# The pool mixer's bias by one matmul per bank, and GpSimd's tensor operations moved to VectorE

## The chip, the cores and the metric

The kernel runs on one core of one Trainium2 chip. The metric is device time in microseconds (us): the time of an execution of the whole program. The profile shows one execution by the hardware profiler; its span reaches from the first to the last instruction. The engines are PE (TensorE, matmuls), with its weight loads as PEld; DVE (VectorE); ACT (ScalarE); POOL (GpSimd); SP (SyncE), which issues the DMAs.

## The reference

One layer of a decoder trunk over x of 1024 tokens by 1024 columns, float32:

```python
h = rms_norm(x, norm_mix_g)                  # per token
for gi, w_len in enumerate((2, 4, 8, 16)):   # 4 groups of 256 columns
    d[gi] = mean of h over the last w_len tokens - h     # fewer at the start
y = scale * (einsum('bsgc,gcd->bsgd', d, pool_w) + pool_b)
x = x + y
f = (silu(gate) * val) @ ffn_w_out           # val, gate: halves of
                                             # causal_conv3(rms_norm(x, norm_ffn_g) @ ffn_w_in) + conv_b
out = x + f                                  # hidden width 2816 (twice)
```

The change concerns the term `scale * pool_b` in y, and sums on the way to the first feed-forward product.

## The kernel before, in words

The tokens go in eight tiles of 128. A loop of twelve passes (j = 0 to 11) is a software pipeline over them. In pass j it writes:

- mixer_norm(j): the window matrices, scaled by the tile's 1/rms (DVE, L148).
- mixer_window(j - 1): 8 matmuls of 128x128 (L152, each shown as two) give the windowed differences in PSUM (psd). A correction of the first 16 tokens (L187, L189), then a split into a rounded part dh (ACT, L190) and a rest dl (DVE, L191). Between them stands L181: GpSimd adds the scaled bias to the tile xs[j] itself, in place, once the window matmuls have read it.
- in pass 1 also mixer_edges (the 16 tokens ahead of each tile) and mixer_weights: pool weights times gain and scale (DVE, L168, 8 pieces), split into wph (ACT, L173) and wpl (DVE, L174).
- mixer_out(j - 2): 24 matmuls of 128x256 (L206) into psy, two banks: per group of 256 columns six matmuls, dh by wph, dh by wpl, dl by wph, for two halves of the contraction. Then L209 (DVE) adds psy and xs[j]; the sum x1 is stored to DRAM (L210), its statistics are taken (L131 to L138, ACT and DVE), and a diagonal matrix of 1/rms is built (L213).
- ffn_operand(j - 4): 8 matmuls of x1 by that diagonal (L229, each shown as two) transpose and scale the tile; seven of eight column blocks are brought out by ACT (L234), one by DVE (L236), into n2f. The first feed-forward product is a Strassen-Winograd scheme, so it needs sums of quarters of n2f. Tiles 0 to 3 are only split (L251 on ACT, L252 on DVE). For tiles 4 to 7 the difference b11 = b12 - b11 is formed (DVE, L263) and split as operand T1, and two more differences, b12 = b22 - b12 (L246) and b21 = b21 - b22 (L247), are formed by GpSimd.

The statistics of the coming tiles, preparation steps for the first product's left operands (prep_event, with splits by L69 and L70 and sums by L263 and L266) and its first three products (event) are written into the same loop. load_in(0) and load_in(1), which bring w_in, stand in passes 4 and 6. After the loop come the operands B22, T2, T3 and T4; for T4, GpSimd adds t1 to t4 in two halves (L432). Then all 22 blocks of the first product run, seven products of 12 matmuls of 128x512 each (L295), and then the second product (L567), 924 matmuls of 128x512.

GpSimd's other work is at the start: memsets and masks of the window matrices (L88 to L103), and L121, which multiplies the bias rows, brought to all partitions by a DMA (L117), by the scale rows (L112).

The order on each engine is not that of the text alone. The framework plans it when the kernel is built, from the order of writing, its own costs and the buffers that are free; the waits are put in by it. Each engine then runs its queue in that order. `issue_after(marks[...])` keeps some preparation steps behind L209 of a given tile. float32 is multiplied as two or three products of parts rounded to fp32r, which is why tensors are split into a rounded part and a rest.

Of the kernel before, what the change touches and what calls it, by code (L numbers as in the profile page):

```python
# [7 lines left out]
F32 = mybir.dt.float32  # L8
F32R = mybir.dt.float32r
BF16 = mybir.dt.bfloat16  # L10
AF = mybir.ActivationFunctionType
ALU = mybir.AluOpType
PSUM = bass.MemoryType.PSUM

P = 128
# [8 lines left out]
WINDOWS = (2, 4, 8, 16)  # L24
HALO = 16
EPS = 1e-6
# Columns of the packed per-partition parameters: conv taps, conv bias, gains of the norms.
CW, CB, GM = 0, 3 * 2 * NF, 4 * 2 * NF
GF = GM + NK
NPAR = GF + NK  # L30
# Columns of the packed constants: identity, factors of the first rows, windows of the first tile.
FAC = P
B0 = FAC + 2 * NG * HALO
BD = B0 + NG * P
# Operands of the first product that are ready before the mixer ends; columns of the second norm's gain that ScalarE applies.
NOPS_A = 3
ACT_GAIN = 7

# [5 lines left out]
def trunk_kernel(ctx: ExitStack, tc: tile.TileContext, x, consts, par, rows, pool_w, w_in, w_out, out):  # L44
# [16 lines left out]
    def raw_tile(name):  # L61
        return work.tile([P, 2, D], F32, tag="raw", name=name, bufs=2)
# [7 lines left out]
        nc.vector.tensor_tensor(t[:, 1, :], src, t[:, 0, :].bitcast(F32), ALU.subtract)  # L70
        return t

# [1 line left out]
    xs = {}  # L74

    def load_x(j):
# [12 lines left out]

    nc.gpsimd.memset(x_edge[:HALO, :], 0.0)  # L90
    for g, w in enumerate(WINDOWS):
        # Row (j, r) is x[128 j - 16 + r], column (j', t) is token 128 j' + t: 1 / w where j == j' and r - 16 > t - w
        e = edge_band[:, g, :].rearrange("p (j t) -> p j t", t=HALO)
        nc.gpsimd.memset(edge_band[:, g, :], 1.0 / w)
        affine(e, e, ALU.is_gt, 0.0, w - HALO, [[-HALO, NS], [-1, HALO]], 1)
        affine(e, e, ALU.is_ge, 0.0, HALO - 1, [[HALO, NS], [0, HALO]], -1)
    for g, w in enumerate(WINDOWS):
        # 1 / w where s - w < s' <= s, less 1 where s' == s
        m = band[:, g, :]
        nc.gpsimd.memset(m, 1.0 / w)  # L100
        affine(m, m, ALU.is_ge, 0.0, 0, [[1, P]], -1)
        affine(m, m, ALU.is_gt, 0.0, w, [[-1, P]], 1)
        affine(m, m, ALU.not_equal, 1.0 / w - 1.0, 0, [[1, P]], -1)  # L103
    par_sb = const.tile([P, NPAR], F32, tag="par", name="par_sb")
    wp_raw = raw_tile("wp_raw").rearrange("p a (c d) -> p (a c) d", d=GRP)
    scale_b = raw_tile("scale_b")[:, 0, :]
    bias_b = pp.tile([P, D], F32, tag="bias_b", name="bias_b")
    load_x(0)
    nc.sync.dma_start(cst, consts)
    nc.sync.dma_start(x_edge[HALO:, :], x.rearrange("(j r) d -> j r d", r=P)[: NS - 1, P - HALO :, :])  # L110
# [7 lines left out]
    for j in range(3, NS):  # L118
        load_x(j)

    nc.gpsimd.tensor_tensor(bias_b, bias_b, scale_b, ALU.mult)  # L121
    eps_t = const.tile([P, 1], F32, tag="eps", name="eps_t")
    nc.vector.memset(eps_t, EPS)
    ident = cst[:, :FAC]
# [3 lines left out]
    def rstd_of(src, name):  # L128
        junk = pp.tile([P, D], BF16, tag="junk", name=f"junk_{name}")
        st = pp.tile([P, 4], F32, tag="st", name=f"st_{name}", bufs=8)  # L130
        nc.scalar.activation(junk, src, AF.Square, accum_out=st[:, 0:1])  # L131
        nc.scalar.activation(st[:, 1:2], st[:, 0:1], AF.Sqrt, bias=eps_t, scale=1.0 / D)
        nc.vector.tensor_scalar(st[:, 0:1], st[:, 0:1], 1.0 / D, EPS, op0=ALU.mult, op1=ALU.add)
        nc.vector.reciprocal(st[:, 2:3], st[:, 1:2])
        # One Newton step on 1 / sqrt
        nc.vector.scalar_tensor_tensor(st[:, 3:4], st[:, 2:3], st[:, 0:1], st[:, 2:3], op0=ALU.mult, op1=ALU.mult)  # L136
        nc.vector.tensor_scalar(st[:, 3:4], st[:, 3:4], -0.5, 1.5, op0=ALU.mult, op1=ALU.add)
        nc.vector.tensor_tensor(st[:, 2:3], st[:, 2:3], st[:, 3:4], ALU.mult)  # L138
        return st[:, 2:3]
# [10 lines left out]
    def windows(ps, src, weights):  # L150
        for c in range(NK):
            nc.tensor.matmul(ps[:, c * P : (c + 1) * P], src[:, c * P : (c + 1) * P], weights[:, c // 2, :], start=True, stop=True)  # L152

    edges = pp.tile([P, NK, P], F32, tag="edges", name="edges")

    def mixer_edges():
# [1 line left out]
        windows(ps, x_edge, edge_band)  # L158
        nc.scalar.activation(edges, ps.rearrange("p (c s) -> p c s", c=NK), AF.Copy)

# [1 line left out]
    wph = pp.tile([P, 2 * NG, GRP], F32R, tag="wph", name="wph")  # L162
    wpl = pp.tile([P, 2 * NG, GRP], F32R, tag="wpl", name="wpl")

# [13 lines left out]
    def mixer_window(j):  # L178
        ps = bank2(f"psd{j}")
        windows(ps, xs[j], bands.pop(j))  # L180
        nc.gpsimd.tensor_tensor(xs[j], xs[j], bias_b, ALU.add)  # L181
        dh = pp.tile([P, NK, P], F32R, tag="dh", name=f"dh{j}", bufs=2)
        dl = pp.tile([P, NK, P], F32R, tag="dl", name=f"dl{j}", bufs=1)
        ps3 = ps.rearrange("p (c s) -> p c s", c=NK)
        first = ps3[:, :, :HALO]
        if j == 0:
            nc.vector.tensor_tensor(first, first, fac, ALU.mult)  # L187
        else:
            nc.vector.tensor_tensor(first, first, edges[:, :, j * HALO : (j + 1) * HALO], ALU.add)  # L189
        nc.scalar.activation(dh, ps3, AF.Copy)  # L190
        nc.vector.tensor_tensor(dl, ps3, dh.bitcast(F32), ALU.subtract)  # L191
        ds[j] = (dh, dl)
# [4 lines left out]
    def mixer_out(j):  # L197
        dh, dl = ds.pop(j)
        ps = bank2(f"psy{j}")
        for g in range(NG):  # L200
            o = ps[:, g * GRP : (g + 1) * GRP]
            n = 0
            for k in range(2):
                c = 2 * g + k
                for a, w in ((dh, wph), (dh, wpl), (dl, wph)):
                    nc.tensor.matmul(o, a[:, c, :], w[:, c, :], start=n == 0, stop=n == 5)  # L206
                    n += 1
        x1 = xs.pop(j)
        marks[j] = nc.vector.tensor_tensor(x1, ps, x1, ALU.add).ins  # L209
        nc.sync.dma_start(x1_dram[j * P : (j + 1) * P, :], x1)  # L210
        r = rstd_of(x1, f"b{j}")
        diag = pp.tile([P, P], F32, tag="diag", name=f"diag{j}", bufs=2)
        nc.vector.tensor_scalar(diag, ident, r, None, op0=ALU.mult)  # L213
        n2s[j] = (x1, diag)
# [10 lines left out]
    def ffn_operand(j):  # L225
        x1, diag = n2s.pop(j)
        ps = bank2(f"pst{j}")
        for c in range(NK):
            nc.tensor.matmul(ps[:, c * P : (c + 1) * P], x1[:, c * P : (c + 1) * P], diag, start=True, stop=True)  # L229
        cols = slice(j * P, (j + 1) * P)  # L230
        ps3 = ps.rearrange("p (c s) -> p c s", c=NK)
        gain = par_sb[:, GF : GF + NK]
        for c in range(ACT_GAIN):
            nc.scalar.activation(n2f[:, c, cols], ps3[:, c, :], AF.Identity, scale=gain[:, c : c + 1])  # L234
        rest = slice(ACT_GAIN, NK)
        nc.vector.tensor_tensor(n2f[:, rest, cols], ps3[:, rest, :], gain[:, rest].unsqueeze(2).to_broadcast([P, NK - ACT_GAIN, P]), ALU.mult)  # L236
        lo, hi = slice(0, 4), slice(4, 8)
        if j < NS // 2:
            split_n(nops["B11"], n2f[:, lo, cols], cols)
            split_n(nops["B21"], n2f[:, hi, cols], cols)  # L240
            return
        cols0 = slice(cols.start - NH, cols.stop - NH)
        b11, b12, b21, b22 = n2f[:, lo, cols0], n2f[:, lo, cols], n2f[:, hi, cols0], n2f[:, hi, cols]
        sub(b11, b12, b11)
        split_n(nops["T1"], b11, cols0)
        nc.gpsimd.tensor_tensor(b12, b22, b12, ALU.subtract)  # L246
        nc.gpsimd.tensor_tensor(b21, b21, b22, ALU.subtract)  # L247

    def split_n(t, src, cols=slice(None), ks=slice(None)):
        h = t[:, 0, ks, cols]  # L250
        nc.scalar.activation(h, src, AF.Copy)  # L251
        nc.vector.tensor_tensor(t[:, 1, ks, cols], src, h.bitcast(F32), ALU.subtract)  # L252

# [1 line left out]
    order = [j + k * NP2 for j in range(NP2) for k in range(2)]  # L255
    raws, sums, aops = {}, {}, {}

# [114 lines left out]
        if p == "P4":  # L372
            gated(n)

# [1 line left out]
    def stat(j):  # L376
        if j in xs and j not in stats:
            stats[j] = rstd_of(xs[j], f"a{j}")
# [2 lines left out]
    for j in range(NS + 4):  # L381
# [7 lines left out]
        if j == 1:  # L389
            mixer_edges()  # L390
            mixer_weights()
        if 0 <= j - 2 < NS:
            mixer_out(j - 2)
        if 0 <= j - 4 < NS:
# [34 lines left out]
    for ks in halves:  # L429
        split_n(nops["T3"], t3[:, ks], ks=ks)  # L430
    for ks in halves:
        nc.gpsimd.tensor_tensor(t4[:, ks], t4[:, ks], t1[:, ks], ALU.add)  # L432
        split_n(nops["T4"], t4[:, ks], ks=ks)
    mid.close()
    late_stack = ExitStack()
# [2 lines left out]
        event(k)  # L438
    late_stack.close()

# [1 line left out]
    fin = ctx.enter_context(tc.tile_pool(name="fin", bufs=1))  # L442
    free = []

    def take(name):
        """Room for [P, 512] of float32, where the first product's operands were."""
        if not free:
            take.n += 1
            if take.n <= 2:
# [64 lines left out]
    starts = []  # L514

    def z_start(name, i, rows_, cols):
        """x1's block plus the first product."""
        z = zs[name, i] = z_tile(name, i)
        r = rows_ * NH + i * P
        nc.sync.dma_start(z, x1_dram[r : r + P, s_half[cols]])  # L520
        add(z, z, zs["q1", i])
# [15 lines left out]
    for k in range(-SLOOK, len(oevents)):  # L537
# [14 lines left out]
        if f == 0 and opens:  # L552
            for i in range(4):
                tag = ("XXYY" if set_ == "X" else "YZZZ")[i]
                pool = ps_x if tag == "X" else ps_yz
                obanks[set_, i] = pool.tile([P, NH], F32, tag=tag, name=f"o{p}{i}")
        # The last blocks of the last product go bank by bank, so that all banks but one leave early
        if k >= len(oevents) - TAIL:
            if f < NP2 - 1:
                continue  # L560
# [33 lines left out]


def constants():
    """What the windows' shapes alone decide."""
    import numpy as np

    r, t, h = np.arange(P)[:, None], np.arange(P), np.arange(HALO)  # L600
# [39 lines left out]
```

## Time and profile before

| | |
|---|---|
| device time, median of 3 runs | 739.74 us (738.17 to 740.25) |
| span of the profiled execution | 736.8 us |
| mean granted PE clock | 0.991 |
| PE busy | 700.1 us (95%) |
| DVE busy | 627.6 us (85%) |
| ACT busy | 352.3 us (48%) |
| POOL busy | 48.0 us (7%) |

The profiled execution has a span of its own, 736.8 us; the device time of the runs includes what lies before and after the span, 2.9 us at the median. In rows of the timeline the columns are start, duration, engine, line, operation, output and inputs, shape and count; in brackets the engine's idle time before it and what ended it. Rows of groups have the count behind an x, then busy us and mean ns of one, then the idle time before. Rows of one line or tile have the least, median and longest duration in ns. Rows of a stretch have the busy time and number of instructions of each engine, then the granted PE clock as a share of full speed, the busy share of the DMA engines and what they moved. An engine's durations overlap by some hundredths, since an instruction starts before the one ahead of it has written out everything.

### The profile page before, as it was taken

To read this page: it belongs to the slowest core of one execution; us is meant where nothing else is said; L and a number is where in the kernel's file an instruction comes from. 1 tells how busy PE (TensorE), PEld (TensorE's weight loads), DVE (VectorE), ACT (ScalarE), POOL (GpSimd) and SP (SyncE) were. 2 spreads that over 40 slices of the span, in tenths; PEclk is the share of its full clock that TensorE was granted. 3 is DMA by queue.
4 is the path that set the end of the run, shared out by engine and by line. 5 is a ranking of instruction groups with operands and counts; after the bars stand their busy time and mean duration, and the time that the engine had idled before them with its cause. 6 is when DMAs were issued, how large, how long until landed. Compare 5 with 4: busy or idle time off the path is not lost.

```text
span 736.8 us, 8791 instructions
## 1 busy us (share of the span) xinstructions
PE 700.1 (95%) x3236; PEld 579.9 (79%) x3236; DVE 627.6 (85%) x928; ACT 352.3 (48%) x565; POOL 48.0 (7%) x52
## 2 busy tenths in 40 slices
PE   4688869999999999999999999999999999999997
PEld 3688857888888888888888888888887788888886
DVE  3899999999988888888888888877996898698993
ACT  5478654645444444444444444444543344444441
POOL 4523360000000000000000000000000000000000
PEclk9899989999999999999999999999999999999999
DMA  9531103133222222112122222226988920005341
GB/s 280 199 144 57 59 0 115 35 133 119 86 82 67 80 86 81 67 67 80 79 86 86 86 85 87 86 85 210 329 298 291 321 93 1 0 1 171 101 157 57
DMA packets 30882, 83.83 MB, mean 114 GB/s; under 512 B 3335, under 2 KB 4487, under 8 KB 28023
## 3 DMA queue, kind: packets, MB, share of 16 engines
q1 hardware_dynamic: 30839, 83.28, 32.3%
q8 instruction: 25, 0.41, 0.2%
q14 instruction: 18, 0.15, 0.1%
HBM read 63.34 MB, written 19.92 MB: 113 GB/s over the span
## 4 chain that ended last, share of the span: by engine, by line
PE 73%; DVE 14%; DMA 8%; issue 2%; ACT 2%; SPq 1%; DVEq 0%; ACTq 0%
PE Y L295 23%; PE oP L567 21%; PE Z L295 14%; PE X L295 14%; DMA blk<-g_dram 3%; DMA blk<-in_w_out_dram 2%; DMA x<-in_x_dram 1%; DVE T L252 1%; DVE wp_raw L168 1%; PE psy L206 1%; DMA B21s<-in_w_out_dram 1%; DVE x L209 1%; DVE dl L191 1%; DMA A12s<-g_dram 1%; DVE st_b L136 1%
## 5 line engine op out<-in xcount | busy, mean ns | idle before, releaser
L567 PE MATMUL oP<-oBP,oAP 128*128 128x512 f32 x924 | 211.3, 390 | 2.6 <-DVE oBP L70 1.7
L567 PEld LDWEIGHTS oP<-oBP,oAP 128*128 128x128 f32 x924 | 173.1, 188 | 40.6 <-DVE oBP L70 3.1
L295 PE MATMUL Z<-T,S1s 128*128 128x512 f32 x264 | 66.7, 403 | 4.4 <-DVE T L252 3.0
L295 PE MATMUL Z<-B,S4s 128*128 128x512 f32 x264 | 64.1, 392 | 1.5 <-ACT S3s L69 1.5
L295 PE MATMUL Y<-T,S3s 128*128 128x512 f32 x264 | 64.5, 393 | 0.6 <-DVE q L324 0.6
L295 PE MATMUL X<-B,A11s 128*128 128x512 f32 x264 | 64.6, 393 | 0.0
L295 PE MATMUL Y<-T,S2s 128*128 128x512 f32 x264 | 64.3, 392 | 0.0
L295 PEld LDWEIGHTS Z<-T,S1s 128*128 128x128 f32 x264 | 51.0, 194 | 16.9 <-DVE T L252 3.3
L295 PE MATMUL Y<-T,A22s 128*128 128x512 f32 x264 | 64.0, 391 | 0.0
L295 PE MATMUL X<-B,A12s 128*128 128x512 f32 x264 | 63.4, 389 | 0.0
L295 PEld LDWEIGHTS Z<-B,S4s 128*128 128x128 f32 x264 | 49.4, 188 | 12.9 <-ACT S3s L69 1.9
L295 PEld LDWEIGHTS Y<-T,S3s 128*128 128x128 f32 x264 | 49.5, 188 | 12.1 <-DVE q L324 1.0
L295 PEld LDWEIGHTS Y<-T,S2s 128*128 128x128 f32 x264 | 49.6, 188 | 11.2
L295 PEld LDWEIGHTS X<-B,A11s 128*128 128x128 f32 x264 | 49.4, 188 | 11.2
L295 PEld LDWEIGHTS Y<-T,A22s 128*128 128x128 f32 x264 | 49.6, 188 | 10.8
L295 PEld LDWEIGHTS X<-B,A12s 128*128 128x128 f32 x264 | 49.5, 188 | 10.3
L69 ACT ACTIVATE oBP<-blk 128x512 fp32r<-128x512 f32 x32 | 20.2, 633 | 46.9 <-PE oP L567 41.6
L353 ACT ACTIVATE gate<-gate 128x1024 f32<-128x1024 f32 x22 | 23.4, 1062 | 39.6 <-DVE gate L344 39.6
L343 DVE SCALAR_TENSOR_TENSOR val<-ha,par_sb,val 128x1023 f32<-128x1023 f32 x22 | 28.2, 1283 | 12.7 <-ACT val L342 12.7
L335 DVE TENSOR_TENSOR ha<-Z,q 128x512 f32<-128x512 f32 x20 | 13.8, 691 | 24.7 <-PE Z L295 24.7
L342 ACT ACTIVATE gate<-hb,par_sb 128x1024 f32<-128x1024 f32 x22 | 27.4, 1246 | 14.5 <-DVE hb L337 14.4
L342 ACT ACTIVATE val<-ha,par_sb 128x1024 f32<-128x1024 f32 x22 | 27.4, 1244 | 13.4 <-DVE ha L335 4.2
(128 smaller groups left out, 1130.2 us busy)
## 6 DMA issues: line engine op xcount, KB each, us to landing
win<-in_w_in_dram SPq DMA_DIRECT2D x22, 1024.0 KB, 4.8
g_dram<-val SPq DMA_DIRECT2D x22, 512.0 KB, 2.6
blk<-g_dram SPq DMA_DIRECT2D x33, 256.0 KB, 5.4
blk<-in_w_out_dram SPq DMA_DIRECT2D x31, 256.0 KB, 5.5
A12s<-g_dram SPq DMA_DIRECT2D x22, 256.0 KB, 4.5
B21s<-in_w_out_dram SPq DMA_DIRECT2D x22, 256.0 KB, 3.4
x<-in_x_dram SPq DMA_DIRECT2D x8, 512.0 KB, 10.5
x_dram<-x SPq DMA_DIRECT2D x8, 512.0 KB, 2.8
```

The source lines that it names most:

```text
L69: nc.scalar.activation(t[:, 0, :], src, AF.Copy)
L136: nc.vector.scalar_tensor_tensor(st[:, 3:4], st[:, 2:3], st[:, 0:1], st[:, 2:3], op0=ALU.mult, op1=ALU.mult)
L168: nc.vector.scalar_tensor_tensor(wp_raw[:, c, :], scale_b[:, g * GRP : (g + 1) * GRP], par_sb[:, GM + c : GM + c + 1], wp_raw[:, c, :], op ...
L191: nc.vector.tensor_tensor(dl, ps3, dh.bitcast(F32), ALU.subtract)
L206: nc.tensor.matmul(o, a[:, c, :], w[:, c, :], start=n == 0, stop=n == 5)
L209: marks[j] = nc.vector.tensor_tensor(x1, ps, x1, ALU.add).ins
L295: nc.tensor.matmul(bank, a[:, i, ks], b[:, l, k, :], start=opens and m == 0, stop=m == 11, skip_group_check=not opens)
L335: tt(hid[n, "a"][:, NH:], bank, hid[n, "q2"], ALU.add)
L342: nc.scalar.activation(t, src, AF.Identity, bias=par_sb[:, CB + f : CB + f + 1], scale=w[2])
L343: nc.vector.scalar_tensor_tensor(t[:, 1:], src[:, : S - 1], w[1], t[:, 1:], op0=ALU.mult, op1=ALU.add)
L353: nc.scalar.activation(gate, gate, AF.Silu)
L567: nc.tensor.matmul(obanks[set_, i], a[:, u, i * P : (i + 1) * P], b[:, v, :], start=opens and g == 0 and m == 0, stop=g == NP2 - 1 and m = ...
```

## The change

GpSimd keeps its memsets and masks and loses all of L121, L181, L246, L247 and L432.

- The bias rows are loaded into the second half of the buffer that holds the scale rows, instead of a tile of their own.
- mixer_bias, new, is written once in pass 1, behind mixer_weights. It sets a 128x128 tile mean_w to 2/128 (DVE), multiplies bias by scale (DVE, 128x1024), rounds that to bias_hl on all 128 rows (ACT), and overwrites rows 64 to 127 of bias_hl with the rest (DVE).
- mixer_out adds, per bank of 512 columns, one matmul of 128x512 with mean_w as the stationary operand and bias_hl as the moving one: 64 equal rows times 1/64 of the rounded part, and 64 times 1/64 of the rest, so that every token gets scale times bias. The 24 other matmuls stay in the same order; only the first of a bank has start set, and the bias matmul, last in its bank, has stop.
- L246 and L247 become DVE subtractions, L432 a DVE addition, at the same places of the text.

```diff
-    scale_b = raw_tile("scale_b")[:, 0, :]
-    bias_b = pp.tile([P, D], F32, tag="bias_b", name="bias_b")
+    rows_b = raw_tile("rows_b")
+    scale_b, bias_b = rows_b[:, 0, :], rows_b[:, 1, :]
...
-    nc.gpsimd.tensor_tensor(bias_b, bias_b, scale_b, ALU.mult)
...
+    bias_hl = pp.tile([P, D], F32R, tag="bias_hl", name="bias_hl")
+    mean_w = pp.tile([P, P], F32R, tag="mean_w", name="mean_w")
+
+    def mixer_bias():
+        nc.vector.memset(mean_w.bitcast(F32), 2.0 / P)
+        nc.vector.tensor_tensor(bias_b, bias_b, scale_b, ALU.mult)
+        nc.scalar.activation(bias_hl, bias_b, AF.Copy)
+        low = slice(P // 2, P)
+        nc.vector.tensor_tensor(bias_hl[low, :], bias_b[low, :], bias_hl[low, :].bitcast(F32), ALU.subtract)
...
-        nc.gpsimd.tensor_tensor(xs[j], xs[j], bias_b, ALU.add)
...
-        for g in range(NG):
-            o = ps[:, g * GRP : (g + 1) * GRP]
-            n = 0
-            for k in range(2):
-                c = 2 * g + k
-                for a, w in ((dh, wph), (dh, wpl), (dl, wph)):
-                    nc.tensor.matmul(o, a[:, c, :], w[:, c, :], start=n == 0, stop=n == 5)
-                    n += 1
+        for h in range(2):
+            cols = slice(h * NH, (h + 1) * NH)
+            for c in range(4 * h, 4 * h + 4):
+                o = ps[:, c // 2 * GRP : (c // 2 + 1) * GRP]
+                for i, (a, w) in enumerate(((dh, wph), (dh, wpl), (dl, wph))):
+                    nc.tensor.matmul(o, a[:, c, :], w[:, c, :], start=c % 4 == 0 and i == 0, stop=False, skip_group_check=True)
+            nc.tensor.matmul(ps[:, cols], mean_w, bias_hl[:, cols], start=False, stop=True, skip_group_check=True)
...
-        nc.gpsimd.tensor_tensor(b12, b22, b12, ALU.subtract)
-        nc.gpsimd.tensor_tensor(b21, b21, b22, ALU.subtract)
+        sub(b12, b22, b12)
+        sub(b21, b21, b22)
...
             mixer_weights()
+            mixer_bias()
...
-        nc.gpsimd.tensor_tensor(t4[:, ks], t4[:, ks], t1[:, ks], ALU.add)
+        add(t4[:, ks], t4[:, ks], t1[:, ks])
```

## The prediction

> **What bounds the kernel now.** I read the page's head first, then the busy time by stretches (the span cut where L209 adds tiles 0, 2 and 7), then what PE waited for, then GpSimd's groups, and last the timeline of VectorE beside GpSimd.
>
> ```profile
> span 736.8 us, 8791 instructions
> ```
>
> The runs shown have a median of 739.74 us, so 2.9 us lie around the span; I take them as unchanged. I work in the span's time and carry the difference over to the median.
>
> ```profile
> core 0: us, PE busy (x) PEld busy (x) DVE busy (x) ACT busy (x) POOL busy (x), PEclk, DMA share, GB/s
> 20.00:33.20 13.20, 6.59 (x42) 6.20 (x41) 12.06 (x20) 3.49 (x7) 6.82 (x4) 0.74 0.50 190
> 33.20:42.94 9.74, 8.98 (x74) 8.78 (x75) 7.70 (x25) 7.57 (x15) 4.57 (x2) 1.00 0.57 209
> 42.94:82.16 39.22, 35.45 (x284) 33.78 (x282) 37.29 (x82) 28.83 (x73) 12.79 (x6) 1.00 0.18 70
> 82.16:123.00 40.84, 32.55 (x145) 25.50 (x144) 40.84 (x49) 23.15 (x48) 15.13 (x9) 0.92 0.17 65
> 123.00:140.00 17.00, 17.00 (x76) 13.93 (x75) 16.98 (x22) 9.25 (x11) 0.00 (x0) 1.00 0.04 14
> ```
>
> In the last row PE has no gap and GpSimd nothing to do: whatever the change does, it does before 123 us, and what it saves there moves all later work forward by as much. Before that there are four stages. In the fill (20 to 33.2) and the drain (82.16 to 123) VectorE is all but full while PE is half or four fifths busy. In the middle, two rows, PE itself has 8.98 of 9.74 and 35.45 of 39.22 us. So a lighter VectorE is worth much at the two ends and little in between. What PE waited for says the same:
>
> ```profile
> PE psy L206 <- DVE wpl L174: 6.3, 1, 6.3
> PE Z L295 <- DVE T L252: 3.0, 1, 3.0
> ```
>
> The first is the wait for the split pool weights, in the fill; the second for the operand T1 of the last tiles, in the drain. Both name VectorE. Why VectorE is late there is seen by laying GpSimd's work beside it:
>
> ```profile
> L181 POOL TENSOR_TENSOR x<-x,bias_b 128x1024 f32<-128x1024 f32 x8 | 19.4, 2433 | 31.6 <-PE psd L152 26.2 <-ACT n2f L234 5.4
> L247 POOL TENSOR_TENSOR n2f<-n2f 128x512 f32<-128x512 f32 x4 | 6.5, 1626 | 0.0
> ```
>
> L246 has the same form as L247; L432 and L121 are like L181, twice and once. Now one of them in the timeline, and beside it the range of L138 (least, median and longest in ns):
>
> ```profile
> L138 DVE TENSOR_TENSOR st_a<-st_a x8: 145/154/2184, 7.8 to 62.8; 128x1 f32<-128x1 f32 x8
> ```
>
> ```profile
> 32.98 2.40 POOL L181 TENSOR_TENSOR x<-x,bias_b 128x1024 f32<-128x1024 f32 x1 [6.30 <-PE psd L152]
> 33.20 1.22 DVE L209 TENSOR_TENSOR x<-psy,x 128x1024 f32<-128x1024 f32 x1
> ...
> 54.58 2.41 POOL L181 TENSOR_TENSOR x<-x,bias_b 128x1024 f32<-128x1024 f32 x1 [5.77 <-PE psd L152]
> ...
> 54.82 2.18 DVE L138 TENSOR_TENSOR st_a<-st_a 128x1 f32<-128x1 f32 x1
> ```
>
> The product of two single columns takes 0.15 us as a rule and 2.18 us at 54.82, where it starts under a GpSimd addition and ends with it (54.58 + 2.41 = 56.99; 54.82 + 2.18 = 57.00). The addition at 33.20, which takes one input from PSUM, runs its 1.22 us beside GpSimd. So a VectorE operation with both inputs in SBUF stands still until GpSimd's two-input operation is over, and holds VectorE's queue (a tensor_scalar as well, L213 below). I count those stalls and set the moved work against them.
>
> **The change part by part.** *The fill.*
>
> ```profile
> L168 DVE SCALAR_TENSOR_TENSOR wp_raw<-scale_b,par_sb,wp_raw x8: 465/475/2587, 15.0 to 27.9; 128x256 f32<-128x256 f32 x8
> ```
>
> ```profile
> L174 DVE TENSOR_TENSOR wpl<-wp_raw,wph x4: 678/687/2690, 18.0 to 29.1; 128x512 fp32r<-128x512 f32 x4
> ```
>
> ```profile
> 18.61 5.87 DVE L168 SCALAR_TENSOR_TENSOR wp_raw<-scale_b,par_sb,wp_raw 128x256 f32<-128x256 f32 x4
> 19.00 2.72 POOL L121 TENSOR_TENSOR bias_b<-bias_b,scale_b 128x1024 f32<-128x1024 f32 x1 [10.68 <-DMA bias_b<-in_rows_dram]
> ...
> 21.79 4.88 POOL L181 TENSOR_TENSOR x<-x,bias_b 128x1024 f32<-128x1024 f32 x2
> ```
>
> Four weight products cost 5.87 us where 4 x 0.47 = 1.9 would do: 4.0 lost. One weight split costs 2.69 instead of 0.69: 2.0 lost. Together 6.0 us, under L121 and the first two L181. All three go from GpSimd. What comes instead, once, is mixer_bias: on VectorE a memset of a 128x128 tile, the product bias times scale (128x1024) and the subtraction on 64 rows (64x1024); on ScalarE one copy to fp32r (128x1024).
>
> ```profile
> L263 DVE TENSOR_TENSOR n2f<-n2f x6: 675/681/1210, 77.2 to 113.1; 128x512 f32<-128x512 f32 x4, 128x1024 f32<-128x1024 f32 x2
> ```
>
> ```profile
> L190 ACT ACTIVATE dh<-psd x8: 1002/1004/1024, 14.8 to 72.4; 128x1024 fp32r<-128x1024 f32 x8
> ```
>
> The product is a 1.21, the longest of L263's row; its 0.68 is the price of 128x512. The subtraction has half the rows: between 0 and 1.21; I take 1.21, because the row has as many elements per partition. The memset lies between 0 and one 128x128 operation, which the 0.68 for four times as much bounds; I take 0.1. The copy is the 1.00 of L190; ScalarE is busy 3.49 of 13.20 us here, so its queue has room, but between product and subtraction it is a hop of 1.0 us, and the next tile's statistics and dh, queued behind the copy, wait with it for the product. The product waits for the bias rows, which came at 19.00 (the row of L121): what is queued on VectorE behind it waits too, if the planner sets it earlier than that. The bias rows now lie in the buffer of the scale, so the second load of w_in can take it only after the subtraction; load_in(1) is written five passes of the tile loop later, and these passes cover it. Without them it would be late by the chain above, some 3 us.
>
> The first mixer_out is the place where this bites. PE takes its queue in order, and the bias product of columns 0 to 511 stands ahead of the twelve matmuls of the other half, of the windows queued after them, and so of L191 and L209 of the next tile. If product and subtraction come last on VectorE, the fill regains 6.0 - 1.2 - 1.2 = 3.6 us; if they lie in VectorE's waits for ScalarE's weight copies, all 6.0. I take 4.5, nearer to the lower end, since the hop over ScalarE comes on top.
>
> The granted clock of this stage is 0.74, with the long wait in it: of PE's 6.59 us, 6.59 x 0.26 = 1.7 would go at full clock. I leave that out of the sum and put it in the range. The Trainium skill (TensorE: Matmul & The Clock Gate, Part 1) says that PE falls to half rate after about 3.4 us of idleness; the row agrees, and by that rule a wait cut below this length would return the whole 1.7, for a time 1.7 us lower than mine.
>
> *The middle.* Every tile loses its L181 and gains two matmuls of 128x512.
>
> ```profile
> 144.62 2.76 PE Y L295 x12
> ```
>
> Twelve such take 2.76 us, 0.23 each: 0.46 a tile, 3.7 over eight tiles. The weight load of the constant tile lies beside a running matmul as the others do. From 33.20 to 42.94 PE's 8.98 grow by two tiles, 0.92, to 9.90 against 9.74: I take 0 saved (-0.3 to 0.3). From 42.94 to 82.16 five tiles make 35.45 + 2.3 = 37.8 of 39.22: at most 1.4 saved, however much VectorE is relieved. I take 1.0 (-1 to 1.4). The stalls here, 2.0 us a tile, mostly give VectorE slack that PE can't use. L181's wait for PE and the wait of L209 for it vanish, at no cost.
>
> *The drain.*
>
> ```profile
> L213 DVE TENSOR_SCALAR diag<-cst,st_b x8: 277/287/1285, 41.3 to 87.5; 128x128 f32<-128x128 f32 x8
> ```
>
> ```profile
> 87.49 1.28 DVE L213 TENSOR_SCALAR diag<-cst,st_b 128x128 f32<-128x128 f32 x1
> 88.69 1.77 DVE L252 TENSOR_TENSOR T<-n2f,T 128x512 fp32r<-128x512 f32 x1
> ...
> 91.19 2.38 DVE L263 TENSOR_TENSOR win<-win 128x512 f32<-128x512 f32 x2
> 93.49 1.77 DVE L252 TENSOR_TENSOR T<-n2f,T 128x512 fp32r<-128x512 f32 x1
> ...
> 97.79 1.76 DVE L70 TENSOR_TENSOR S4s<-win,S4s 128x512 fp32r<-128x512 f32 x1
> 99.48 1.75 DVE L252 TENSOR_TENSOR T<-n2f,T 128x512 fp32r<-128x512 f32 x1
> 101.15 2.86 DVE L70 TENSOR_TENSOR S4s<-win,S4s 128x512 fp32r<-128x512 f32 x1
> 103.94 2.86 DVE L70 TENSOR_TENSOR S2s<-win,S2s 128x512 fp32r<-128x512 f32 x1
> ```
>
> Against 0.29 for L213 and 0.68 apiece for the others these lose 1.0, 1.1, 1.0 (two in 2.38), 1.1, 1.1, 1.1, 2.2 and 2.2: 10.8 us. To VectorE come six of the eight L246 and L247 (two lie in the stage before) at 0.68, 4.1, and two L432 at 1.21, 2.4: 6.5 with their full durations, about 5.9 when the tail of each lies under the next (101.15 to 103.94 is 2.79 for a row of 2.86). VectorE is full here, so the drain regains 10.8 - 5.9 = 4.9 us. PE leaves room: 40.84 - 32.55 = 8.3 idle. What is late next is the order: up to 101.15, where the last T1 is ready, 6.4 of stalls go, and if all six differences stand in front of it 4.1 come, 2.3 net; if they stand behind, 6.4. I take 4.9 for the stage, with 2.3 to 6.4.
>
> The sum: 4.5 + 0 + 1.0 + 4.9 = 10.4 us. 739.7 - 10.4 = 729.3. By the ends, 3.6 - 0.3 - 1 + 2.3 = 4.6 gives 735.1, and 6.0 + 1.7 (clock) + 0.3 + 1.4 + 6.4 = 15.8 gives 723.9.
>
> **The rivals.** *PE becomes the bound from 20 us on.* Its idle time in the four stages is 6.6 + 0.8 + 3.8 + 8.3 = 19.5; the low clock costs the 1.7 of the fill and 32.55 x 0.08 = 2.6 more; less 3.7 for the bias products, 20.1 saved: 719.6. For it: VectorE, the only engine that PE waits long for, is freed of 6.0 + 10.8 + 5 x 2.0 = 27 us of stalls. Against it: a tile's chain of statistics stays, and the drain's VectorE is full even without stalls.
>
> *A wash.* The bias chain holds the first tile as long as the stalls did (fill 0), the middle loses 1 to PE's added work, and the differences stand ahead of T1, 2.3, after which PE is short of other operands: 738 to 740, say 738.4. For it: PE's order, and a planner whose order I don't know. Against it: the wait of 6.3 would need bias rows ready near 30 us, 11 after they land.
>
> *VectorE overloaded, slower.* The long rows are no stalls by GpSimd but waits that fall together with it, and stay. Then VectorE carries the moved work on top where it is full: 2.5 in the fill and 5.9 in the drain, 739.7 + 8.4 = 748.1. It decides if, with GpSimd still, L213 or L252 keep rows above 1 us. Against it: ends that agree to 0.01 us, and the untouched 1.22 of L209. The Trainium skill (Perfetto Trace Analysis, Optimizing Scalar/DVE Operations) advises to take work off a saturated VectorE, to GpSimd even, and this change does the opposite; it adds that the two share a read port, so that this might not help, and the rows at 54.58 bear that out.
>
> **How the numbers follow.** Forecast 0.73, PE as bound 0.15, wash 0.07, overload 0.05. About 0.3%, 2.2 us, can be told from no change. The forecast's own range, 723.9 to 735.1, and the PE bound are faster: 0.88; the wash is the same: 0.07; slower: 0.05. The range goes down to the PE bound, rounded to 720, and up to 736, with a little for stages that don't add up.
>
> **What would show it.** No GpSimd row after the masks; VectorE's L168, L174, L213, L252 at their short durations; PE's wait for wpl below 3 us, with a wait of PE for bias_hl in its place at most as long; the addition of tile 0 near 28.7 instead of 33.20; tiles in the middle no faster than 0.3 us each; the last T1 near 89 to 93 instead of 101.2; PE without gaps from about 113. I am wrong if the middle gains over 2 us, if PE's first wait stays above 5, or if VectorE's long rows remain.

## The result, and the profile after

The changed kernel takes 721.99 us (median of 4 runs, 720.44 to 723.45), the kernel before 739.68 us on the same chip: a ratio of 0.9778, with a 95% interval of 0.9758 to 0.9798. That is 17.7 us less, where 10.4 were forecast; the time lies in the stated range of 720 to 736, but below the 723.9 to which the forecast's own terms reach. The profiled execution took 723.45 us with a span of 721.7, so 1.75 us lie around the span. Two disturbed executions of one experiment below (e3) are left out, its profile among them, so that its median is 732.4 us and not the 732.7 of all five, which a text on record below uses; its kernel was profiled again as e11.

Many lines have other numbers in the changed kernel: L138 is L137, L148 is L147, L152 is L151, L168 is L178, L174 is L184, L191 is L200, L206 is L214, L209 is L217, L213 is L221, L229 is L237, L252 is L260, L263 is L271, L295 is L303, L432 is L441. Busy time by stretches of the changed kernel, again cut where tiles 0, 2 and 7 are added:

```profile
core 0: us, PE busy (x) PEld busy (x) DVE busy (x) ACT busy (x) POOL busy (x), PEclk, DMA share, GB/s
20.00:31.33 11.33, 8.07 (x50) 7.33 (x48) 8.57 (x24) 5.14 (x9) 0.00 (x0) 0.85 0.83 313
31.33:41.34 10.01, 9.88 (x80) 9.71 (x81) 6.78 (x22) 8.76 (x18) 0.00 (x0) 1.00 0.32 128
41.34:75.75 34.41, 34.41 (x278) 33.45 (x277) 29.86 (x88) 27.09 (x71) 0.00 (x0) 1.00 0.20 77
75.75:113.00 37.25, 34.86 (x175) 28.59 (x174) 37.25 (x58) 23.27 (x48) 0.00 (x0) 1.00 0.19 71
113.00:130.00 17.00, 16.98 (x73) 13.13 (x72) 17.00 (x22) 11.10 (x15) 0.00 (x0) 1.00 0.08 31
```

GpSimd has nothing to do. In the third row PE has no gap at all, and yet the stretch takes 34.41 us where it took 39.22. In the fourth PE idles 2.4 us instead of 8.3, while VectorE is still full. What PE still waits for, in the changed kernel from 18 to 140 us (total, times, longest):

```profile
PE psd L151 <- DVE bandr L147: 3.7, 2, 2.7
PE Y L303 <- DVE T L260: 1.0, 1, 1.0
PE psy L214 <- DVE dl L200: 0.7, 1, 0.7
PE X L303 <- DVE A11s L70: 0.7, 1, 0.7
PE Z L303 <- DVE r L337: 0.6, 1, 0.6
```

The waits of 6.3 for wpl and 3.0 for T1 are gone. VectorE's stalled operations are back at their plain durations; their rows by line (least, median and longest in ns), and the last splits of T1 in the timeline:

```profile
L178 DVE SCALAR_TENSOR_TENSOR wp_raw<-rows_b,par_sb,wp_raw x8: 466/474/478, 15.7 to 22.4; 128x256 f32<-128x256 f32 x8
```

```profile
L184 DVE TENSOR_TENSOR wpl<-wp_raw,wph x4: 670/679/680, 18.7 to 24.0; 128x512 fp32r<-128x512 f32 x4
```

```profile
L221 DVE TENSOR_SCALAR diag<-cst,st_b x8: 275/280/286, 38.0 to 81.1; 128x128 f32<-128x128 f32 x8
```

```profile
85.09 0.68 DVE L260 TENSOR_TENSOR T<-n2f,T 128x512 fp32r<-128x512 f32 x1
...
87.83 0.69 DVE L260 TENSOR_TENSOR T<-n2f,T 128x512 fp32r<-128x512 f32 x1
```

The longest L168 was 2587 ns, the longest L174 2690, the longest L213 1285. The last T1 is ready at 88.5 instead of 101.2.

To see where the 15.1 us of the spans come from, one more point is needed: the last copy of `ha`, which ends the first product for PE. First the kernel before, then the changed one (the last start stands behind "to"):

```profile
L321 ACT ACTIVATE ha<-X x22: 581/600/602, 97.6 to 511.0; 128x512 f32<-128x512 f32 x22
```

```profile
L329 ACT ACTIVATE ha<-X x22: 577/600/647, 87.6 to 497.9; 128x512 f32<-128x512 f32 x22
```

| point | before | after | gained up to here | gained in the stage | forecast |
|---|---|---|---|---|---|
| addition of tile 0 | 33.20 | 31.33 | 1.9 | 1.9 | 4.5 |
| addition of tile 2 | 42.94 | 41.34 | 1.6 | -0.3 | 0 |
| addition of tile 7 | 82.16 | 75.75 | 6.4 | 4.8 | 1.0, at most 1.4 |
| last T1 ready | 101.2 | 88.5 | 12.7 | 6.3 | 2.3 to 6.4 |
| last copy of `ha` | 511.0 | 497.9 | 13.1 | 0.4 | with the row above, 4.9 |
| end of the span | 736.8 | 721.7 | 15.1 | 2.0 | 0 |

The last row, the second product, is no effect that I can put down to the change: from the last `ha` to the end the spans of all profiles here, in which that part of the program is the same, take 222.8 (e9) to 225.8 us (the kernel before), and the changed kernel 223.8. The other 2.6 us, between 15.1 and 17.7, come from which execution was profiled: that of the changed kernel was the slowest of its four (723.45, 1.5 above the median), and the kernel before, with 1.75 us around its span, would have taken 738.6 in its profile, 1.1 below its median.

### The profile page after: what moved, and what is told of

Read it like the earlier page. It is cut to its first block, busy times and chain, and to the rows that moved or that the text cites. A ratio compares the mean times of both kernels' runs of the same rounds, so it can differ in the third digit from the quotient of the medians.

```text
span 721.7 us, 8803 instructions
## 1 busy us (share of the span) xinstructions
PE 698.9 (97%) x3252; PEld 580.2 (80%) x3252; DVE 609.7 (84%) x941; ACT 352.3 (49%) x566; POOL 7.7 (1%) x33
## 4 chain that ended last, share of the span: by engine, by line
PE 80%; DVE 11%; DMA 6%; issue 1%; SPq 1%; ACT 1%; DVEq 0%; ACTq 0%
PE Y L303 23%; PE oP L576 21%; PE X L303 15%; PE Z L303 15%; PE psy L214 3%; DMA blk<-g_dram 3%; PE psd L151 2%; DMA x<-in_x_dram 1%; PE pst L237 1%; DVE n2f L271 1%; DVE oBP L70 1%; DVE T L260 1%; DMA blk<-in_w_out_dram 1%; DVE blk L271 1%; DVE oAP L70 1%
## 5 line engine op out<-in xcount | busy, mean ns | idle before, releaser
L303 PE MATMUL X<-B,A11s 128*128 128x512 f32 x264 | 65.6, 394 | 0.7 <-DVE A11s L70 0.7
L303 PE MATMUL Y<-T,S2s 128*128 128x512 f32 x264 | 65.1, 394 | 1.1 <-DVE T L260 1.0
L303 PE MATMUL Z<-B,S4s 128*128 128x512 f32 x264 | 64.1, 392 | 0.6 <-DVE r L337 0.6
L303 PE MATMUL Z<-T,S1s 128*128 128x512 f32 x264 | 64.6, 393 | 0.0
L303 PE MATMUL Y<-T,S3s 128*128 128x512 f32 x264 | 64.3, 392 | 0.0
L303 PE MATMUL Y<-T,A22s 128*128 128x512 f32 x264 | 64.1, 392 | 0.0
L303 PE MATMUL X<-B,A12s 128*128 128x512 f32 x264 | 63.4, 390 | 0.0
L303 PEld LDWEIGHTS Y<-T,S2s 128*128 128x128 f32 x264 | 49.2, 188 | 13.2 <-DVE T L260 1.5
L303 PEld LDWEIGHTS X<-B,A11s 128*128 128x128 f32 x264 | 49.3, 188 | 12.3 <-DVE A11s L70 1.1
L303 PEld LDWEIGHTS Z<-B,S4s 128*128 128x128 f32 x264 | 49.5, 188 | 11.8 <-issue 1.1
L303 PEld LDWEIGHTS Z<-T,S1s 128*128 128x128 f32 x264 | 49.5, 188 | 11.4 <-ACT S1s L69 0.2
L303 PEld LDWEIGHTS Y<-T,S3s 128*128 128x128 f32 x264 | 49.6, 188 | 11.2
L303 PEld LDWEIGHTS Y<-T,A22s 128*128 128x128 f32 x264 | 49.5, 188 | 11.1 <-ACT val L350 0.3
L303 PEld LDWEIGHTS X<-B,A12s 128*128 128x128 f32 x264 | 49.5, 188 | 10.3
L69 ACT ACTIVATE S4s<-win 128x512 fp32r<-128x512 f32 x22 | 13.9, 633 | 40.4 <-PE Z L303 35.9
## 6 DMA issues: line engine op xcount, KB each, us to landing
x<-in_x_dram SPq DMA_DIRECT2D x8, 512.0 KB, 10.4
```

The costliest lines, as they stand in the source:

```text
L69: nc.scalar.activation(t[:, 0, :], src, AF.Copy)
L303: nc.tensor.matmul(bank, a[:, i, ks], b[:, l, k, :], start=opens and m == 0, stop=m == 11, skip_group_check=not opens)
```

## The experiments

Every run is compared with the kernel before on its own chip, where that took 736.9, 738.1 and 737.1 us in the three groups (e1 to e4; e5, e6, e8, e9; e7, e10, e11, e13).

| run | what it is | us | ratio to before, 95% interval |
|---|---|---|---|
| e1 | bias by PE, sums on GpSimd | 729.4 | 0.9890 (0.9864 to 0.9916) |
| e2 | bias on GpSimd, sums on VectorE | 730.5 | 0.9904 (0.9878 to 0.9930) |
| e3 | changed, two idle additions per tile on GpSimd | 732.4 | 0.9933 (0.9907 to 0.9958) |
| e4 | changed, four memsets per tile on GpSimd | 722.0 | 0.9795 (0.9767 to 0.9824) |
| e5 | changed, bias added by VectorE | 721.5 | 0.9778 (0.9752 to 0.9805) |
| e6 | changed, no bias at all | 716.6 | 0.9714 (0.9681 to 0.9748) |
| e7 | changed, mixer_bias in pass 2 | 722.0 | 0.9790 (0.9765 to 0.9815) |
| e8 | changed, bias rows loaded early | 722.1 | 0.9785 (0.9763 to 0.9808) |
| e9 | changed, one idle addition per tile on GpSimd | 725.7 | 0.9834 (0.9813 to 0.9855) |
| e10 | changed, tiles 0 and 1 on VectorE | 722.3 | 0.9795 (0.9774 to 0.9816) |
| e11 | e3 once more | 733.1 | one run |
| e13 | changed, L432 on GpSimd | 725.6 | 0.9838 (0.9812 to 0.9864) |

### e1 and e2: the two halves

```diff
 # e1: the changed kernel with
-        sub(b12, b22, b12)
-        sub(b21, b21, b22)
+        nc.gpsimd.tensor_tensor(b12, b22, b12, ALU.subtract)
+        nc.gpsimd.tensor_tensor(b21, b21, b22, ALU.subtract)
...
-        add(t4[:, ks], t4[:, ks], t1[:, ks])
+        nc.gpsimd.tensor_tensor(t4[:, ks], t4[:, ks], t1[:, ks], ALU.add)
 # e2: the kernel before with the same lines the other way round
```

> Half of the change: the bias by PE, while GpSimd keeps the differences (L246, L247) and the sum (L432). Theory A (GpSimd operations that read SBUF hold VectorE up, each where it runs): the fill and the middle keep what they gained in the changed kernel's trace, 1.9 + 4.5 us, and the drain loses its 6 to 7, so about 733 us, and VectorE's L260 keeps rows above 1 us. Theory B (the middle was bound by PE, as predicted, and the gain past 10 us came from the drain): a gain of at most 2.9, so 737 or more.

> The other half: differences and sum on VectorE, the bias still added by GpSimd. Theory A: only the drain gains, 6 to 7 us, so about 733 us, and the two halves add up to the whole change within 2 us. Theory B: the drain alone brings over 10 us, so 729 or less.

The bias alone gives 1.1%, the sums alone 0.96%; together 2.06%, against 2.22% for the whole change, so they add up. Both theories counted their times from 739.7 us, and the kernel before took 736.9 on this chip. Counted from there, theory A gives about 730.5 for either half, and 729.4 and 730.5 came. Theory B, the prediction's own picture, falls: e1 gains 7.5 us, more than the 2.9 that B allows, and e2 6.4, less than its 10. In e1 the middle (39.92 to 74.86) takes 34.94 us, nearly as short as in the changed kernel, and the old wait for T1 stays; in e2 the middle (43.51 to 81.72) takes 38.21 and the old wait for wpl stays, at 4.6 instead of 6.3. PE's longest wait in e1, and in e2:

```profile
PE Z L303 <- DVE T L260: 3.0, 1, 3.0
```

```profile
PE psy L206 <- DVE wpl L174: 4.6, 1, 4.6
```

### e3, e4, e9 and e11: GpSimd work for nothing

```diff
-        windows(ps, xs[j], bands.pop(j))
+        used = bands.pop(j)
+        windows(ps, xs[j], used)
+        for _ in range(2):                                        # e3, e11; once in e9
+            nc.gpsimd.tensor_tensor(used, used, band, ALU.add)
+        # e4 instead: four times nc.gpsimd.memset(used, 0.0)
```

> The changed kernel, and per tile two GpSimd additions of 128x512 whose result nobody uses, in place in the tile's window matrices after the window matmuls have read them. They read SBUF twice. Theory A (a GpSimd operation that reads SBUF holds up VectorE operations with two SBUF inputs): about 2 us of VectorE per tile stand still again, rows of L135 or L137 above 1 us come back, and the middle gives back its 4 to 5 us: 726 to 728. Theory C (the gain came from the removed wait of the addition L209 for GpSimd and from another order, not from a lock): 722, within 1.

> As the run before, but with four GpSimd memsets of 128x512 per tile in the same place, which write SBUF and read nothing. Theory A in its narrow form (only reads collide): 722, within 1, and no VectorE row stretched. In its wide form (any GpSimd work collides): 726 to 728, as with the additions.

> The changed kernel with one idle GpSimd addition of 128x512 per tile instead of two. Theory A: half the loss of the run with two (10.8 us), about 727, and in the profile single VectorE operations of 128x1 or 128x512 with two SBUF inputs stretched by up to 1.3 us, none with a PSUM input. Theory G (the loss with two came from the window matrices being held longer): less than 2 us, 722 to 724, and no stretched rows.

> The kernel with two idle GpSimd additions per tile once more, for its profile: it took 732.7 us, 10.8 over the changed kernel, where one addition took 3.7 over it. Theory A: the stalls of VectorE are 16 times up to 1.3 us, and past the first of them a tile's slack is used up, so the middle (tile 2 to tile 7) is longer than 34.4 us by 5 or more. Theory J (the surplus lies in the fill, where the window matrices are held): the middle is within 2 us of 34.4.

Nobody uses these results, no addition waits for them, and still one addition per tile costs 0.5% and two cost 1.4%, some three fifths of what the whole change gains. Memsets of nearly the same length (four of 128x512 in 2.44 us, where two additions take some 2.7) cost nothing that can be measured. So theory C, a removed wait or another order, falls. So does theory G, that the window matrices are held longer: the memsets hold them as well. What costs is that GpSimd reads. A GpSimd operation with a single input was not tried. The collision in e9, VectorE's row and then GpSimd's:

```profile
52.86 0.15 DVE L133 RECIPROCAL st_b<-st_b 128x1 f32<-128x1 f32 x1
52.93 1.18 DVE L137 TENSOR_TENSOR st_a<-st_a 128x1 f32<-128x1 f32 x1
```

```profile
52.80 1.29 POOL L192 TENSOR_TENSOR bandr<-bandr,band 128x512 f32<-128x512 f32 x1 [5.49 <-PE psd L151]
```

The reciprocal, one input, runs its 0.15 us under the GpSimd addition; the product of two columns starts 0.07 later and ends with it. With two additions per tile the scaling of the window matrices, one tensor by a column, is held too (e11, with GpSimd's row first; 0.47 is its plain duration), and the same line beside the memsets of e4 only a little:

```profile
48.16 2.73 POOL L193 TENSOR_TENSOR bandr<-bandr,band 128x512 f32<-128x512 f32 x2 [4.52 <-DVE diag L224]
48.30 1.44 DVE L147 TENSOR_SCALAR bandr<-band,st_a 128x512 f32<-128x512 f32 x1
```

```profile
48.41 2.44 POOL L193 MEMSET bandr<- 128x512 f32 x4 [4.39 <-PE psd L151]
48.48 0.74 DVE L147 TENSOR_SCALAR bandr<-band,st_a 128x512 f32<-128x512 f32 x1
49.14 0.13 DVE L136 TENSOR_SCALAR st_b<-st_b 128x1 f32<-128x1 f32 x1
49.19 0.28 DVE L201 TENSOR_TENSOR psd<-psd,edges 128x128 f32<-128x128 f32 x1
49.39 0.14 DVE L137 TENSOR_TENSOR st_b<-st_b 128x1 f32<-128x1 f32 x1
```

There the last row, with two SBUF inputs, runs its 0.14 us in the middle of the memsets (48.41 to 50.85). The Trainium skill (SBUF — State Buffer, Who interferes with whom) tells these apart in the same way: a VectorE operation with two SBUF inputs collides with a GpSimd operation that reads SBUF, not with one that only writes, and a tensor_scalar in a mode that uses both ports collides with any.

The sizes came out otherwise than expected. One addition cost 3.7 us where 5 were expected, two cost 10.4 where 4 to 6 were. In e11 the stretch from tile 2 to tile 7 takes 38.99 us, 4.6 over the changed kernel: less than theory A's 5 and more than theory J's 2. The addition of tile 0 comes at 35.37, 4.0 later than in the changed kernel's profile. In e9 the middle takes 35.25, only 0.8 more: the stalls of one addition mostly fit into the slack that PE leaves VectorE there. Most of what e9 loses lies ahead of it, where tile 0 comes at 33.30, 2.0 later. The fill can be taken apart. PE restarts at the windows of tile 2 and then has the same 30 matmuls up to the addition of tile 0:

| run | PE restarts | tile 0 added | us between | granted clock |
|---|---|---|---|---|
| e4 | 24.39 | 28.95 | 4.56 | 1.00 |
| changed | 25.22 | 31.33 | 6.11 | 0.72 |
| e9 | 26.33 | 33.30 | 6.97 | 0.61 |
| e11 | 28.27 | 35.37 | 7.10 | 0.60 |

PE's restart, 1.1 us later in e9 and 3.05 in e11, follows from VectorE rows stretched by the idle additions. In e9 they are an L135 at 13.22 (0.64 for 0.22) and an L184 at 21.41 (1.34 for 0.68), 1.1 us in all; in e11 they are L135 and L137 at 13.09 and 14.09, and L184 and L135 at 22.62 and 23.61, 2.9 us in all. The rest, 0.9 and 1.0 us, goes with the lower granted clock. Why the clock differed is not shown.

### e5 and e6: what the bias costs, by PE or by VectorE

```diff
 # e5 and e6: without the bias matmuls, and the last of the other matmuls of a bank stops it
-            nc.tensor.matmul(ps[:, cols], mean_w, bias_hl[:, cols], start=False, stop=True, skip_group_check=True)
 # e5, in mixer_window behind the windows; mixer_bias is the product alone, and the bias rows have a tile of their own
+        add(xs[j], xs[j], bias_b)
 # e6: nothing for it, no bias rows are loaded, and there is no mixer_bias
```

> The changed kernel with the bias added to the tile by VectorE, one addition of 128x1024 per tile at the place where GpSimd had it, and no bias matmuls. Theory A2 (without GpSimd the middle is bound by PE, which the bias matmuls lengthen by 0.46 a tile, and VectorE had 4.5 of 34.4 us to spare there): five additions of 1.2 take 6 us, more than VectorE has to spare, so VectorE becomes the bound again: 723 to 727. Theory D (VectorE has room, and the matmuls are pure cost): 718 to 720.

> The changed kernel without the bias: no bias rows loaded, no mixer_bias, no bias matmuls (the term scale times bias is left out). Theory A2: PE is full in the middle, so its 7 matmuls pairs there come off in full, about 3 us, and the fill loses the bias product in front of the window matrices of tile 2, up to 2 us: 717 to 719. Theory D': PE's added matmuls lie beside VectorE's work and cost nothing: 721 to 722.

The whole bias costs 722.0 - 716.6 = 5.4 us by PE, and the same within the interval when VectorE adds it: both of my ranges for e5 missed, and e6 came out 0.4 below theory A2's 717 to 719. The middle rows of e6 and e5, from tile 2 to tile 7:

```profile
38.48:70.56 32.08, 32.08 (x267) 31.49 (x266) 29.13 (x82) 27.20 (x71) 0.00 (x0) 1.00 0.21 83
```

```profile
38.14:72.96 34.82, 33.70 (x278) 32.81 (x277) 33.48 (x84) 28.40 (x72) 0.00 (x0) 1.00 0.19 76
```

In e6 PE is full and the middle is 34.41 - 32.08 = 2.33 us shorter, ten matmuls at 0.23: PE is the bound of the middle, and each matmul counts in full. In e5 PE has 1.1 us of gaps and VectorE 33.48 of 34.82: VectorE nearly becomes the bound, and the middle comes out 0.4 longer than by PE, which its fill makes up (tile 0 is added at 27.39). So the gain of the change comes from what GpSimd no longer does, and not from PE's cheaper addition.

### e13: the sum of the drain alone

```diff
-        add(t4[:, ks], t4[:, ks], t1[:, ks])
+        nc.gpsimd.tensor_tensor(t4[:, ks], t4[:, ks], t1[:, ks], ALU.add)
```

> The changed kernel with only the last sum, L432 of the kernel before, back on GpSimd (two additions of 128x1024, late in the drain). Theory H (the drain is decided when the last T1 is ready; behind it PE is full, and VectorE's stalls are covered): 722, within 1. Theory I (every stall of VectorE in the drain counts): 4.4 us of stalls come and 2.3 of additions go, so 724.

It costs 0.5%, more than either theory allowed. VectorE and GpSimd in e13, and PE behind them:

```profile
89.74 5.69 DVE L271 TENSOR_TENSOR win<-win 128x512 f32<-128x512 f32 x2
95.36 1.21 DVE L260 TENSOR_TENSOR B<-n2f,B 128x1024 fp32r<-128x1024 f32 x1
```

```profile
89.38 5.51 POOL L441 TENSOR_TENSOR n2f<-n2f 128x1024 f32<-128x1024 f32 x2 [81.07 <-ACT B L259]
```

```profile
PE Z L303 <- ACT S4s L69: 3.7, 1, 3.7
```

The planner could set the sum early, and it fell on two subtractions (1.28 without it) whose results ScalarE and then PE wait for: 4.4 us of stall became 3.7 of PE's wait, and the last `ha` came at 501.3, 3.4 later. Theory H is wrong that VectorE's stalls are covered behind T1. Behind that wait the granted clock was lower too: PE's 24 matmuls of Z by S4s took 8.19 us at 0.68, where the changed kernel has 5.93 of PE time for them at 1.00. Three waits of the changed kernel behind this point, of 0.6 to 1.0 us each, are absent in return. How much a stall costs hangs on what stands behind it.

### e7, e8 and e10: the fill

```diff
 # e7: in the loop over passes
-            mixer_bias()                      # pass 1
+        if j == 2:
+            mixer_bias()
 # e8: the DMA of bias_b behind that of scale_b, mixer_bias() in pass 0 behind edge_norm()
 # e10: tiles 0 and 1 without bias matmuls, add(xs[j], xs[j], bias_b) on VectorE; bias_hl made in pass 3
```

> The changed kernel with mixer_bias written in pass 2, ahead of mixer_out(0) and behind the window matrices of tile 2. Theory E: those matrices no longer wait for the bias product, PE's wait of 2.7 us for them shrinks below 1.5, and 1 us is gained: 720 to 721. Theory F: 722, within 1, because the first mixer_out then waits for the bias instead.

> The changed kernel with the bias rows loaded right behind the scale rows and mixer_bias written in pass 0, so that product, copy and rest are done before the pool weights are. Theory E (in the fill PE waits for the window matrices of tile 2, which stand behind the bias product on VectorE): the fill gains 1 to 2 us, less up to 1.4 for the later arrival of tile 1 and the pool weights: 720 to 722. Theory F (the bias chain costs nothing in the fill): 722 to 724, by the later arrivals.

> The changed kernel with the bias of tiles 0 and 1 added by VectorE and that of tiles 2 to 7 by PE; the rounded bias is made in pass 3, when PE is no longer waiting. Theory E (the fill waits for the bias chain in front of the window matrices of tile 2; with VectorE adding, the first addition came at 27.4 instead of 29 to 31 us): the fill gains 1.5 to 3 us and the middle stays at 34.4: 719 to 721. Theory F (the fill varies by when the DMAs land and by the clock, not by the bias chain): 722, within 1.

All three lie within 0.4 us of the changed kernel. Theory E falls; only its sign in e7, the shorter wait for the window matrices, came. What stands in the way in the changed kernel is seen in the fill, PE first and then VectorE:

```profile
22.28 0.28 PE L214 MATMUL psy<-wph,dl 128*128 128x256 f32 x1
25.22 2.93 PE L151 MATMUL psd<-bandr,x 128*128 128x128 f32 x12 [2.66 <-DVE bandr L147]
27.81 0.77 PE L215 MATMUL psy<-bias_hl,mean_w 128*128 128x512 f32 x1
```

```profile
22.84 1.21 DVE L159 TENSOR_TENSOR rows_b<-rows_b 128x1024 f32<-128x1024 f32 x1
23.97 0.68 DVE L184 TENSOR_TENSOR wpl<-wp_raw,wph 128x512 fp32r<-128x512 f32 x1
```

The planner set the windows of tile 2 into the first mixer_out, ahead of the bias matmul, and they wait for window matrices that stand behind the bias product on VectorE. In e7 that wait shrinks from 2.7 to 1.0, and another of 1.7 for bias_hl comes in its place. In e10 tile 0 is added at 27.05, but tile 2 at 38.72, hardly before e4 (39.02), which has the changed kernel's fill: what tile 0 gains is waited for again two tiles later. No version here beats the changed kernel beyond the interval, except e6, which leaves out part of the sum.

## Why the prediction was right, and where it was wrong

**The mechanism of the stalls was right.** VectorE's long rows were stalls under GpSimd's reads, they went with them, and the time followed. The rival in which they were waits that stay (748.1) is refuted by e3 and e4; the wash by the result. The rival in which PE becomes the bound from 20 us on (719.6) is near the measured time, but not what happened: PE became the bound in the middle only, and VectorE stays full to the end of the drain. The size was not right. The time lies 1.9 us below 723.9, the lower end that the terms give, and is in the stated range only because that was opened down to this rival's figure. As far as the sum goes, that is luck.

**The fill: 1.9 us in the profile, 4.5 forecast.** The wait for the bias chain was foreseen, but at the bias matmul; it came one step ahead of it, at the window matrices of tile 2. A part of the miss is the execution profiled: the table of e4, e9 and e11 shows 6.11 us at a granted clock of 0.72 where e4 took 4.56 at 1.00, and the statistics of the edge tokens, the first VectorE work of this chain, began at 12.91 instead of 12.20 before. Tile 0 was added at 28.95, 29.92 and 30.09 us in e4, e1 and e7, with the same work in the fill or nearly so, which is 4.3, 3.3 and 3.1 earlier than before. But the kernel before lost 1.7 us to the clock here, which the 4.5 did not count. An estimate at full clock for both is 33.20 - 1.7 = 31.5 before and 31.33 - 1.55 - 0.7 (the later start) = 29.1 after: 2.4 us from the relieved VectorE, below the lower end of 3.6. The prediction's condition for the whole 1.7, a wait below some 3.4 us, was met with 2.66, and yet the clock of the changed kernel's row is 0.85, so that 8.07 x 0.15 = 1.2 us of PE's time there still go to it; the condition did not hold as a rule here.

**The middle: the step that failed.** "At most 1.4 saved, however much VectorE is relieved" was wrong; 4.8 were, and by the prediction's own sign (wrong if the middle gains over 2 us) this part of it failed. I had taken PE's busy time, 35.45 us, as work that has to be done in this stretch. Two things were wrong with that. The groups of PE's rows in the middle that differ, of the kernel before and then of the changed one:

```profile
L229 PE MATMUL pst<-diag,x 128*128 128x128 f32 x88 | 11.0, 277 | 2.9 <-DVE n2f L236 2.0 <-DVE st_b L138 0.9
L152 PE MATMUL psd<-bandr,x 128*128 128x128 f32 x64 | 8.1, 280 | 0.8 <-DVE x L209 0.8
```

```profile
L237 PE MATMUL pst<-diag,x 128*128 128x128 f32 x72 | 9.0, 275 | 0.0
L151 PE MATMUL psd<-bandr,x 128*128 128x128 f32 x64 | 7.8, 275 | 0.0
L215 PE MATMUL psy<-bias_hl,mean_w 128*128 128x512 f32 x10 | 4.0, 397 | 0.0
```

First, 16 matmuls of L229 fewer lie in the stretch: 14 that ran ahead of the addition of tile 7 now run behind it, and two more ahead of that of tile 2. In a gapless run 16 take 1.78 us (in the changed kernel from 40.03 to 41.81), so 1.8 us left the stretch, most of it for the drain, where PE has room. Second, busy time holds the tails of matmuls in front of every gap: one of L229 lasts 0.28 us, but in the gapless run the next starts after 0.11. Without gaps the same work is cheaper: the changed kernel's 34.41 us hold no gap, less ten bias matmuls (2.3) they are 32.1 for all but those 16, plus 1.8 makes 33.9 where the rows of before showed 35.45. The difference of 1.55 is a remainder; the seven gaps that the kernel before has in this stretch, with a tail of some 0.16 each, account for 1.1 of it. So the floor was 35.45 - 1.55 - 1.8 + 2.3 = 34.4, and not 37.8. This sum can't test itself, since the 1.55 comes from the measured 34.41; e6 can: its middle has no gap either and takes 32.08, and ten bias matmuls at 0.23, the prediction's price, make 34.4 of it.

**The drain: near in size, in part by luck.** It gained 6.3 us up to the last T1, at the upper end of 2.3 to 6.4, and 0.4 behind it: 6.7 against 4.9. The 6.4 stood for differences that wait behind the last T1. They did not: five of the six stand in front of it in the changed kernel, and by the prediction's prices 6.4 - 5 x 0.68 = 3.0 would have been left. What made up for them is that five other VectorE operations of the same size, three subtractions of `win` and a split each of S1s and S4s, stood in front of the last T1 before and now stand behind it. No term of the forecast has that; it is the planner's order. Behind T1 these five, one difference and the two sums came in where 4.4 us of stalls went. The granted clock of the drain's rows also rose, from 0.92 to 1.00; what that is worth was not separated.

**The span and what lies around it.** I took the 2.9 us between span and median as fixed. In the changed kernel only 1.75 lie there; the rest was the distance of the profiled execution from the median. With the spread of the second product this makes 4.6 of the 17.7 us that no stage before the last `ha` shows. Some of it may be the fill, which came later in this execution than in e1, e4 and e7; that is not shown.

## What to carry to other kernels

In this kernel a GpSimd operation with two SBUF inputs cost not its own time but the time that VectorE's next two-input operation stood still, and all that was queued behind it: look for VectorE rows far above their median that end with a GpSimd row, and add up the surplus. PE's busy time in a stretch with gaps is not a floor; count its matmuls and price them by a gapless run of the same kernel, and let the stretch end where no work crosses it. What takes the place of a GpSimd operation, PE or VectorE, mattered less here (e5) than that GpSimd stopped reading.

## What was not expected of the hardware

GpSimd memsets of some 2.4 us per tile, 17.6 us in all, left two-input VectorE operations alone (0.14 us beside them) and the time too (722.0). Idle additions on GpSimd didn't cost in proportion: 3.7 us for one per tile and 10.4 for two. In the middle the first fit into slack (0.8 us) that the second did not find (4.6); in the fill, 2.0 and 4.0 us later, the stalls counted nearly in full, and a lower granted clock came on top. After a wait of PE of 2.7 us that clock was 0.72 in the changed kernel and 0.61 in e9, so the length of the wait alone does not tell it.
